# A two-layer decoder trunk on one core: a decay matrix from broadcast sums, new ranks in the planner, and weight transfers of one unit

## Chip, core and metric

The kernel runs on one core of one Trainium2 chip. The metric is the device time of one execution in microseconds; the median of three runs of the kernel before is 699.82 us (697.88 to 703.11).

## What is computed

Two decoder layers over 256 tokens of width 1024, and a last RMSNorm. All inputs are float32. Layer 0 mixes with a gated delta rule (8 heads of 64) beside a short gated convolution; layer 1 with sparse attention (16 heads, 4 groups, three branches). Each layer ends in a squared-ReLU MLP of width 4096. Of the reference, the part that the change rewrites:

```python
g = -jnp.exp(a_log) * jax.nn.softplus(a + dt_bias)          # per token and head
gc = jnp.cumsum(chunks(g), axis=-1)
decay = jnp.exp(jnp.where(incl, gc[..., :, None] - gc[..., None, :], -jnp.inf))
m_low = jnp.where(strict, jnp.einsum('nbhik,nbhjk->nbhij', kb, kc) * decay, 0.0)
u = triangular_solve(m_low + eye, vc * bc); w = triangular_solve(m_low + eye, kb * jnp.exp(gc))
attn = jnp.einsum('nbhik,nbhjk->nbhij', qc, kc) * decay
# MLP: jnp.square(jax.nn.relu(h @ w_up)) @ w_down
```

The kernel uses chunks of 128 tokens, so there are two chunks `c` and, per chunk, one decay matrix `E[c]` of 128 x 8 heads x 128.

## The kernel before

**Weights.** All weight matrices lie in one array in the order of use. `_plan` (line 50) lists them as chunks of 512 columns or their like; a chunk consists of units of [128, 1024] float32 (512 KB), the first chunk of half units, the second of units of 528 columns. `loads` (line 435) issues the transfers from SyncE's queue, two units in each, into `stage`, a pool of SB = 4 slots of [128, 2048]; a slot is filled again when both of its units have been split (flag `st`). Two half units of the first chunk share a slot. `x` and the parameter transfers stand between them at fixed positions: `rtab` ahead of transfer RT = 21, the rest of the parameters ahead of transfer P2 = 8. Two streams of `splits` (line 455) turn each unit into a rounded high half `uh` (ScalarE) and a remainder `ul` (VectorE); UB = 4 such pairs exist. The products are then hi x hi, hi x lo, lo x hi: three matmuls of 256 columns for each 128x128 block (`mm256`, line 523), 24 for a unit. `compress` (line 1533) reads its weights straight from the stage.

**The order.** The order of the instructions of every engine is made ahead of time in Python. Work is written as generator streams; at each `yield` a stream names an engine or a flag, and `Order.run` (line 250) takes the stream that can start first by a table of costs, and among equal times the one with the lowest rank (`prio`), then the oldest. `spawn` (line 178) gives a stream without a rank the rank 1 if its parent has rank MAIN (9) or SPLIT, else its parent's. SPLIT is 0 here and CHAIN, the rank of the delta rule's chain (`chain_k`, `chain_main`, `decay`), is 0 too. The stream of projections has rank 9, and -1 while a count of missed matmul columns (`debt`) is above a limit. Attention heads in layer 1 have ranks from 1 up, the ends of the norms 0. `Timed.cost` (line 299) holds the cost table: for rounded float32 the larger of 0.86 ns for each weight column and 0.46 ns for each moving column.

**Layer 0.** The projections k, (z, a, b), v, q, cg, hs, bg run in this order, then the output projection: its blocks 0 to 3 read `yb` (short convolution), 4 to 7 `ya` (delta rule). Beside them runs the chain: `decay` (line 919) makes g; `spans` (line 955) makes E; `chain_k` (line 1057) normalises k and makes `nbk`; `invert` (line 1102) makes `KB` (`keys`), the scores `al` = K KB E (`scores`), and inverts by blocks with `tt`, `uc`, `ys`; `chain_main` (line 1232) solves for x; `output` (line 1277) gives `o` and `ya`. The convolutions of q run on GpSimd, those of k and v on VectorE. The Silu activations of v, q and z wait for the flag `E1`, so that the activation table changes once.

E before: four GpSimd or VectorE products per chunk, triu times a column of g (split into two rounded parts), 128x512 each, and for each half of the heads one bfloat16 matmul that adds the mask `nleb` and two matmuls with `strictr` as weights. ScalarE takes Exp of 128x512 from PSUM.

Of the kernel before, what the change touches and what calls it, by code (L numbers as in the profile page):

```python
# [10 lines left out]
F32 = mybir.dt.float32  # L11
F32R = mybir.dt.float32r
# [8 lines left out]
T = 256  # L21
# [5 lines left out]
UN = 1024  # L27
# [4 lines left out]
FIRST, XS = (1,) * 8, ((1, 2), (2, 4), (4, 6), (6, 8))  # L32
PK, PW, PR, F1, GZ, ZP, LD, RT, P2 = 1, 0, 1, 1, 1, 1, 1, 21, 8
KPOOL, VPOOL, CVB = (), (), {'conv': 4, 'pool': 2}
CHAIN, TOK_FIRST = 0, False
TICK, BUSY = 10240 / 3, 1500.0
MAIN, SPLIT, SHARE, LIMIT, FLOOR, CAP, SPARE = 9, 0, 0.5, 300, -1500.0, 4000.0, 1
ORDER1 = ('kk', 'q0', 'kc', 'vg', 'cmp', 'q1', 'wo')


# [8 lines left out]

def _plan():  # L50

    w = UN, (2, 2)
    l1 = []
    for k in ORDER1:
        l1 += {'vg': [(560, (2,) * 4)], 'cmp': [(0, (2 * UN,) * 4)], 'wo': [w, w]}.get(k, [w])
    return [(UN // 2, FIRST), (528, (2,) * 4)] + [w] * 7 + [w] * 16 + l1 + [w] * 16


def _layout(i):
# [97 lines left out]
class Order:  # L157
# [28 lines left out]
    def flag(self, name):  # L186
        self.flags.setdefault(name, self._now())
# [62 lines left out]
    def run(self):  # L250
        while self.streams:
            best = None
            for i, s in enumerate(self.streams):
                t, at = self._start(s)
                prio = -1 if s.prio == MAIN and self.debt > self.limit else s.prio
                if t is not None and (best is None or (t, prio, i) < best[0]):
                    best = (t, prio, i), s, at
            assert best, [s.want for s in self.streams]
            _, s, at = best
            w, value = s.want, None  # L260
            if isinstance(w, (str, dict)):
                value = at
            else:
                s.hold = max(s.hold, at)
                if w[0] == 'bank':
                    slot = min(self.banks)
                    self.banks.remove(slot)
                    value = self.get_bank(slot[1])
                    self.held[id(value)] = slot[1], value
# [14 lines left out]
class Timed:  # L284
# [14 lines left out]
    def cost(self, op, a, k):  # L299
        aps = [x for x in list(a) + list(k.values()) if isinstance(x, bass.AP)]  # L300
        size = lambda x: int(np.prod(x.shape[1:]))
        if self.name != 'PE':
            return self.other(op, a, k, aps, size)
        rows = aps[1].shape[0]
        if op == 'transpose':
            return 0.85 * rows, rows * rows / 128
        m, n = size(aps[1]), size(aps[2])
        if aps[2].dtype == F32:
            if m <= 64 and aps[0].start_partition():
                return 8 + 0.7 * m, 0.0  # L310
            return max(1.75 * m, 1.68 * n), 4 * n * rows / 128
        return max((0.86 if aps[2].dtype == F32R else 0.25) * m, 0.46 * n), n * rows / 128

    def other(self, op, a, k, aps, size):
        n = max(size(x) for x in aps)
# [28 lines left out]


BANK = ('bank',)
UB, SB, SPARE1 = 4, 4, 0
SLOTS, PTS = 4, 4
WARM = 9

# [17 lines left out]
def _build(ctx, nc, tc, wts, xin, parin, out, off):  # L368
# [37 lines left out]
    pieces, units, left, raw, place = [], [], [], [], []  # L406
    at = slot = 0
    for n, split in _plan():
        fits = 2 if 0 < n * max(split) <= UN else 1
        for j in range(len(split)):  # L410
            place.append((slot + j // fits, j % fits * UN))
        slot = place[-1][0] + 1
        left += [0] * (slot - len(left))
        for per in split:
            if n:
                units += [(len(pieces), u * n, n) for u in range(per)]
            else:
# [17 lines left out]
    def loads():  # L435
        cut = off['ident'][0]
        before = {P2: [get(par[:, cut:], parin[:, cut:npar], npar - cut, 'par2')],
                  RT: [get(e.rtab, parin[:, npar:].rearrange("p (a t) -> p a t", a=2), 2 * T, 'rtab')]}
        for p, x in zip((1, 2, 3, 4), XS):
            before[p] = [load_x(*x)]  # L440
        head = [get(par[:, :cut], parin[:, :cut], cut, 'par'), load_x(0, 1)]
        before[HEAD] = head + before.get(HEAD, [])
        for p, (pos, k) in enumerate(pieces):
            for g in before.get(p, ()):
                yield from g
            slot, o = place[p]
            if not o:
                if slot >= SB:
                    yield 'flag', f'st{slot - SB}'
                st = stage.tile([128, 2 * UN], F32, name="st")  # L450
            staged[p] = st[:, o:]
            yield from get(st[:, o:o + k], bass.AP(tensor=wts.tensor, offset=wts.offset + pos, ap=[[k, 128], [1, k]]),
                           k, f'ld{p}')

    def splits(first):
        for i in range(first, len(units), 2):
            p, o, n = units[i]
            if i >= UB:
                yield 'flag', f'ud{i - UB}'
            yield 'flag', f'ld{p}'  # L460
# [36 lines left out]
    def late_consts():  # L497
        yield 'flag', 'col0'
        make = lambda nm, dt: const.tile([128, 128], dt, name=nm)
        yield 'G'  # L500
        e.strictr, e.nleb = make("strictr", F32R), make("nleb", BF16)
        e.identb, e.ngeb = make("identb", BF16), make("ngeb", BF16)
        G.tensor_copy(e.identb, ident)
        G.tensor_scalar(e.nleb, P('triu'), -1.0, -NEG, op0=OP.add, op1=OP.mult)
        G.tensor_copy(e.strictr, P('strict'))
        flag('consts')
        yield 'G'
        t = tmp.tile([128, T], F32, name="t", bufs=3)[:, :128]
# [345 lines left out]
def layer0(e, n, nxt):  # L854
# [4 lines left out]
    with ExitStack() as ctx:  # L859
# [59 lines left out]
        def decay():  # L919
# [18 lines left out]
            V.scalar_tensor_tensor(q, q, 2.0, z, op0=OP.add, op1=OP.mult)  # L938
            V.scalar_tensor_tensor(sp, sp, 0.0, q, op0=OP.max, op1=OP.add)
            V.scalar_tensor_tensor(g, sp, -1.0, ea[:, None, :].to_broadcast([128, 2, 8]), op0=OP.mult, op1=OP.mult)  # L940
            gp = [p1.tile([128, 2, 8], F32R, name=f"gp{i}", tag=t) for i, t in enumerate(("lz", "lw"))]
            V.tensor_copy(gp[0], g)
            V.tensor_sub(gp[1], g, gp[0].bitcast(F32))
            flag('g')
            spawn(spans(gp))
            b = yield BANK
            yield 'PE'
            PE.matmul(b[:, :8], triu, g[:, 1], start=True, stop=True)
            PE.matmul(b[:, 8:16], strict, g[:, 0], start=True, stop=True)
            yield 'A'  # L950
            A.activation(eg, b[:, :16], AF.Exp)
            release(b)
            flag('eg')

        def spans(gp):

            yield 'flag', 'consts'
            for c in range(2):
                parts = [m4.tile([128, 8, 128], F32R, name="gt", tag=f"m4{i}") for i in range(2)]
                E[c] = m4.tile([128, 8, 128], F32, name=f"E{c}")  # L960
                for q in range(2):
                    h = slice(4 * q, 4 * q + 4)
                    for i in range(2):
                        spawn(products(parts[i][:, h], gp[i][:, c, h], f'gt{c}{q}{i}'))
                for q in range(2):
                    b = yield BANK
                    d = view(b, 4, 128)
                    yield 'PE'
                    PE.matmul(d, e.identb, e.nleb[:, None, :].to_broadcast([128, 4, 128]), start=True, stop=False)
                    for i in range(2):  # L970
                        yield 'flag', f'gt{c}{q}{i}'
                        yield 'PE'
                        PE.matmul(d, e.strictr, parts[i][:, 4 * q:4 * q + 4], start=False, stop=(i == 1))
                    yield 'A'
                    A.activation(E[c][:, 4 * q:4 * q + 4], d, AF.Exp)
                    release(b)
                flag(f'E{c}')

        def products(dst, col, done):
            pick = yield dict(V=600, G=1076 + DBIAS)  # L980
            (V if pick == 'V' else G).tensor_mul(dst, triu[:, None, :].to_broadcast([128, 4, 128]),
                                                 col.bitcast(F32)[:, :, None].to_broadcast([128, 4, 128]))
            flag(done)


        def pool_conv(dst, pre, w, width):
# [375 lines left out]
        def bg_evac(m, acc):  # L1362
# [1 line left out]
            yield 'flag', 'E1'  # L1364
            yield 'take', 'bg', 2
            if not yb:
                yb.extend(m4.tile([128, 4, T], F32R, name="yb", tag=f"m4{a}") for a in range(2))
            yield 'V'
            t = p2.tile([128, T], F32, name="bgt", tag="lsq")
            V.tensor_mul(t, acc[:, :T], sc['cg'][:, m])  # L1370
# [33 lines left out]
def layer1(e, n, nxt):  # L1404
# [4 lines left out]
    with ExitStack() as ctx:  # L1409
# [123 lines left out]
        def compress():  # L1533
# [1 line left out]
                yield 'flag', f'blocks{i}'  # L1535
            hb = yield BANK
            for k in range(16):
                if k % 4 == 0:
                    w, done = yield from e.whole()
                yield 'PE'  # L1540
                for i in range(2):
                    o = k % 4 * 512 + i * 256
                    PE.matmul(hb[64 * i:64 * i + 64, :256], blk[i][:, k], w[:, o:o + 256], start=(k == 0),
                              stop=(k == 15))
                if k % 4 == 3:
                    flag(done)
            spawn(compressed(hb))

# [312 lines left out]
```

## Time and profile before

| | us |
|---|---|
| median of three runs | 699.82 (697.88 to 703.11) |
| the profiled execution | 699.36 |
| its span, first to last instruction | 697.6 |
| TensorE busy | 664.7 |
| VectorE busy | 479.5 |
| ScalarE busy | 388.1 |
| GpSimd busy | 136.2 |
| mean granted TensorE clock | 0.981 of full speed |

A helper records each instruction, so that all of them carry line 294; rows are told apart by the tiles' names (written tile, then read ones) and by time. Layer 0 ends at about 185 us, its MLP at about 365, layer 1 at about 515. A matmul in float32 appears as two records, one in rounded float32 or bfloat16 as one. A busy share is an average; what counts for an order is which engine waits for which at a given time.

### The profile page before, as it was taken

The numbers are of one execution on the slowest core, as the hardware profiler recorded it, in microseconds if no ns is written. First come the engines' busy times: TensorE is split into PE (matmuls) and PEld (weight loads), VectorE is DVE, ScalarE is ACT, GpSimd is POOL, SyncE is SP. The second block draws the span as 40 slices with busy tenths as digits, with TensorE's granted clock in tenths as the row PEclk, the third lists the DMA queues.
The fourth block names the chain that finished last, engine by engine and source line by source line (L and its number), as shares of the span: only waits on it lengthen the run. The fifth ranks groups of instructions, "written<-read, shape, count | busy, mean of one in ns | idle before, by whom it ended". The sixth has DMA issues, their size and how long they took to land.

```text
span 697.6 us, 15854 instructions
## 1 busy us (share of the span) xinstructions
PE 664.7 (95%) x6573; PEld 625.0 (90%) x6573; DVE 479.5 (69%) x898; ACT 388.1 (56%) x750; POOL 136.2 (20%) x177
## 2 busy tenths in 40 slices
PE   8998879996999999999999999999899999999994
PEld 6997779996999999999999876978699999999994
DVE  6999868674775556566568999997396655555452
ACT  7556223331588787444446567676478878544430
POOL 2035678100210000011013251212130000011121
PEclk9999989997999999999999999999999999999997
DMA  8843331311355555555553367213135555555501
GB/s 296 289 175 136 122 123 64 107 36 55 138 206 190 183 189 203 209 185 182 190 207 110 129 224 290 73 62 122 61 122 182 183 183 195 207 201 182 182 1 60
DMA packets 17640, 109.05 MB, mean 156 GB/s; under 512 B 2080, under 2 KB 2336, under 8 KB 5536
## 3 DMA queue, kind: packets, MB, share of 16 engines
q1 hardware_dynamic: 17280, 107.52, 44.1%
q8 instruction: 51, 0.84, 0.5%
q10 hardware_dynamic: 288, 0.52, 0.2%
q14 instruction: 21, 0.17, 0.1%
HBM read 106.99 MB, written 1.05 MB: 155 GB/s over the span
## 4 chain that ended last, share of the span: by engine, by line
PE 75%; DVE 16%; issue 3%; ACT 3%; DMA 1%; SPq 0%; POOL 0%; DVEq 0%; ACTq 0%; POOLq 0%
PE b L294 75%; DVE ul L294 4%; DVE cvconv L294 1%; DVE x L294 1%; ACT uh L294 1%; DVE kc L294 1%; DMA X<-xt 1%; DVE swq L294 1%; DVE rqt L294 1%; DVE X L294 1%; DVE nm L294 0%; ACT px L294 0%; DVE lc L294 0%; DVE qr L294 0%; DVE cm L294 0%
## 5 line engine op out<-in xcount | busy, mean ns | idle before, releaser
L294 DVE TENSOR_TENSOR ul<-st,uh 128x1024 fp32r<-128x1024 f32 (+3 forms) x204 | 244.2, 1200 | 143.4 <-ACT uh L294 141.1
L294 ACT ACTIVATE uh<-st 128x1024 fp32r<-128x1024 f32 (+3 forms) x204 | 205.8, 1011 | 195.3 <-PE b L294 179.6
L294 PE MATMUL b<-x,uh 128*128 128x256 f32 (+1 forms) x1632 | 295.5, 283 | 2.0 <-DVE x L294 0.8
L294 PEld LDWEIGHTS b<-x,uh 128*128 128x128 f32 x1632 | 249.4, 189 | 6.6 <-ACT uh L294 1.8
L294 PE MATMUL b<-x,ul 128*128 128x256 f32 x832 | 231.1, 279 | 0.7 <-DVE ul L294 0.6
L294 PE MATMUL b<-U,uh 128*128 128x256 f32 x1024 | 174.2, 276 | 0.0
L294 PEld LDWEIGHTS b<-x,ul 128*128 128x128 f32 x832 | 157.1, 189 | 1.8 <-DVE ul L294 1.5
L294 PEld LDWEIGHTS b<-U,uh 128*128 128x128 f32 x1024 | 154.1, 188 | 0.0
L294 PE MATMUL b<-U,ul 128*128 128x256 f32 x512 | 141.3, 276 | 0.0
L294 PEld LDWEIGHTS b<-U,ul 128*128 128x128 f32 x512 | 96.1, 188 | 0.0
L294 POOL TENSOR_TENSOR nacc<-nacc,sq 128x256 f32<-128x256 f32 x24 | 27.1, 1127 | 244.2 <-ACT sq L294 244.1
L294 ACT ACTIVATE px<-b,nm 128x128 f32<-128x128 f32 (+1 forms) x64 | 26.3, 423 | 10.0 <-DVE nm L294 9.7
L294 ACT ACTIVATE U<-u 128x256 fp32r<-128x256 f32 x64 | 26.8, 419 | 2.0
L294 ACT ACTIVATE u<-t 128x256 f32<-128x256 f32 x64 | 26.7, 418 | 2.0
L294 POOL TENSOR_TENSOR px<-px,den 128x128 f32<-128x128 f32 x32 | 17.3, 568 | 53.5 <-DVE den L294 39.1
L294 DVE TENSOR_TENSOR U<-u,U 128x256 fp32r<-128x256 f32 x64 | 27.0, 425 | 0.7 <-ACT U L294 0.7
L294 PE MATMUL b<-uh,x 128*128 128x264 f32 (+1 forms) x128 | 24.9, 290 | 0.0
L294 POOL TENSOR_TENSOR X<-X,par 128x256 f32<-128x256 f32 x8 | 5.5, 694 | 99.2 <-ACT nacc L294 90.2
L294 PE MATMUL b<-ohl,uh 128*128 128x256 f32 x128 | 24.6, 291 | 0.2
L294 ACT ACTIVATE t<-b 128x256 f32<-128x256 f32 x64 | 23.3, 364 | 0.0
L294 DVE SCALAR_TENSOR_TENSOR x<-X,par,x 128x256 fp32r<-128x256 f32 x32 | 19.1, 616 | 4.2 <-ACT x L294 4.1
L294 PEld LDWEIGHTS b<-ohl,uh 128*128 128x128 f32 x128 | 19.6, 189 | 0.9 <-ACT ohl L294 0.3
(274 smaller groups left out, 806.0 us busy)
## 6 DMA issues: line engine op xcount, KB each, us to landing
st<-wts SPq DMA_DIRECT2D x94, 1024.0 KB, 4.8
st<-wts SPq DMA_DIRECT2D x4, 560.0 KB, 3.7
st<-wts SPq DMA_DIRECT2D x4, 528.0 KB, 4.8
st<-wts SPq DMA_DIRECT2D x8, 256.0 KB, 5.4
X<-xt SPq DMA_DIRECT2D x3, 256.0 KB, 5.4
par<-par SPq DMA_DIRECT2D x1, 525.0 KB, 5.8
out_dram<-X SPq DMA_DIRECT2D x2, 256.0 KB, 2.6
out_dram<-X ACTq DMA_DIRECT2D x2, 256.0 KB, 3.1
```

What stands on the lines that cost most here:

```text
L294: r = f(*a, **k)
```

## The change

- E is built otherwise. The column of g for one head, broadcast over 128 columns, is the weights of a float32 matmul with triu as moving operand: every row then holds the running sum of g. The mask matmul stays. Exp is taken head by head with the negated running sum of the row as bias (`ngk`, made by one small ScalarE operation). The products, `strictr` and the split of g go. The two small matmuls for `eg` become one of 16 columns and one of 8. Four `spans` streams are spawned by `decay`.
- The outputs `yb` of the short convolution no longer share their place with the products.
- Ranks: `splits` sets its rank to 0 for the first 16 units and to SPLIT = 0.5 after; so `spawn` now gives the children of rank-0 streams the rank 0. A table YIELD of zeros is added to the start times.
- The cost of a rounded float32 matmul in the planner becomes the larger of 0.885 ns for each weight column and 0.443 ns (up to 256 columns; 0.455 above) for each moving column.
- Each transfer is one unit, and the stage has eight slots of one unit. Two half units of the first chunk share a slot of one unit.

```diff
-MAIN, SPLIT, SHARE, LIMIT, FLOOR, CAP, SPARE = 9, 0, 0.5, 300, -1500.0, 4000.0, 1
+CHAIN, EARLY, TOK_FIRST = 0, 16, False
+YIELD = (0.0, 0.0, 0.0)
+MAIN, SPLIT, SHARE, LIMIT, FLOOR, CAP, SPARE = 9, 0.5, 0.5, 300, -1500.0, 4000.0, 1
...
-    w = UN, (2, 2)
+    w = UN, (1,) * 4
...
-        l1 += {'vg': [(560, (2,) * 4)], 'cmp': [(0, (2 * UN,) * 4)], 'wo': [w, w]}.get(k, [w])
-    return [(UN // 2, FIRST), (528, (2,) * 4)] + [w] * 7 + [w] * 16 + l1 + [w] * 16
+        l1 += {'vg': [(560, (1,) * 8)], 'cmp': [(0, (UN,) * 8)], 'wo': [w, w]}.get(k, [w])
+    return [(UN // 2, FIRST), (528, (1,) * 8)] + [w] * 7 + [w] * 16 + l1 + [w] * 16
...
-        return max((0.86 if aps[2].dtype == F32R else 0.25) * m, 0.46 * n), n * rows / 128
+        return max((0.885 if aps[2].dtype == F32R else 0.25) * m, (0.443 if n <= 256 else 0.455) * n), n * rows / 128
...
-UB, SB, SPARE1 = 4, 4, 0
+UB, SB, SPARE1 = 4, 8, 0
...
-        fits = 2 if 0 < n * max(split) <= UN else 1
+        fits = 2 if 0 < n * max(split) <= UN // 2 else 1
         for j in range(len(split)):
-            place.append((slot + j // fits, j % fits * UN))
+            place.append((slot + j // fits, j % fits * (UN // 2)))
...
-                st = stage.tile([128, 2 * UN], F32, name="st")
+                st = stage.tile([128, UN], F32, name="st")
...
             p, o, n = units[i]
+            order.cur.prio = 0 if i < EARLY else SPLIT
...
-            gp = [p1.tile([128, 2, 8], F32R, name=f"gp{i}", tag=t) for i, t in enumerate(("lz", "lw"))]
-            V.tensor_copy(gp[0], g)
-            V.tensor_sub(gp[1], g, gp[0].bitcast(F32))
-            flag('g')
-            spawn(spans(gp))
             b = yield BANK
             yield 'PE'
-            PE.matmul(b[:, :8], triu, g[:, 1], start=True, stop=True)
-            PE.matmul(b[:, 8:16], strict, g[:, 0], start=True, stop=True)
+            PE.matmul(b[:, :16], triu, g.rearrange("p c h -> p (c h)"), start=True, stop=True)
+            PE.matmul(b[:, 16:24], strict, g[:, 0], start=True, stop=True)
             yield 'A'
-            A.activation(eg, b[:, :16], AF.Exp)
+            ngk = small("ngk", 2, 8)
+            A.activation(ngk.rearrange("p c h -> p (c h)"), b[:, :16], AF.Copy, scale=-1.0)
+            A.activation(eg, b[:, 8:24], AF.Exp)
...
+        def spans(c, q, ngk):
+            b = yield BANK
+            d = view(b, 4, 128)
+            yield 'PE'
+            PE.matmul(d, e.identb, e.nleb[:, None, :].to_broadcast([128, 4, 128]), start=True, stop=False)
+            for j in range(4):
+                yield 'PE'
+                PE.matmul(d[:, j], g[:, c, 4 * q + j:4 * q + j + 1].to_broadcast([128, 128]), triu,
+                          start=False, stop=(j == 3))
+            for j in range(4):
+                yield 'A'
...
+                A.activation(E[c][:, h], d[:, j], AF.Exp, bias=ngk[:, c, h:h + 1])
+            release(b)
...
-                yb.extend(m4.tile([128, 4, T], F32R, name="yb", tag=f"m4{a}") for a in range(2))
+                yb.extend(m4.tile([128, 4, T], F32R, name=f"yb{a}") for a in range(2))
...
-                if k % 4 == 0:
+                if k % 2 == 0:
                     w, done = yield from e.whole()
```

## Rows read from the trace of the kernel before

**Rows 1.** The page, engine totals: busy us, share, instructions.
```profile
PE 664.7 (95%) x6573; PEld 625.0 (90%) x6573; DVE 479.5 (69%) x898; ACT 388.1 (56%) x750; POOL 136.2 (20%) x177
```

**Rows 2.** Stages: stretch, its length, busy us (records) by engine, clock, DMA share, GB/s.
```profile
40.00:70.00 30.00, 26.92 (x213) 24.93 (x214) 28.79 (x63) 16.73 (x30) 15.50 (x13) 1.00 0.34 116
70.00:92.00 22.00, 18.22 (x328) 17.08 (x330) 20.07 (x48) 4.84 (x6) 13.92 (x17) 1.00 0.40 139
92.00:102.00 10.00, 7.54 (x213) 6.81 (x213) 4.00 (x9) 1.89 (x3) 7.76 (x11) 0.66 0.18 41
...
164.00:178.00 14.00, 8.59 (x45) 7.80 (x44) 5.91 (x15) 3.23 (x4) 1.26 (x1) 0.63 0.22 75
```

**Rows 3.** Waits of TensorE, 0 to 180 us: total us, times, longest.
```profile
PE b L294 <- issue: 2.5, 1, 2.5
PE b L294 <- DVE ys L294: 1.9, 1, 1.9
```

**Rows 4.** Order of time, TensorE: start, us, instruction, [idle before, and releaser].
```profile
168.70 1.08 PE L294 MATMUL b<-par,o 128*128 128x128 f32 x4 [4.58 <-DVE o L294]
170.47 1.31 PE L294 MATMUL b<-ya,uh 128*128 128x256 f32 x2 [0.69 <-ACT ya L294]
```

**Rows 5.** Order of time, the chain's start, on VectorE and TensorE.
```profile
54.50 1.01 DVE L294 SCALAR_TENSOR_TENSOR nbk<-beta,rk 128x16 f32<-128x16 f32 x1
57.25 1.06 PE L294 MATMUL b<-par,wide 128*128 128x128 f32 x8 [1.53 <-DVE preconv L294]
71.27 1.27 DVE L294 TENSOR_TENSOR KB<-K,b 128x512 f32<-128x512 f32 x2
78.61 2.15 DVE L294 SCALAR_TENSOR_TENSOR al<-b,rk,E 128x128 f32<-128x128 f32 x8
83.43 0.75 PE L294 MATMUL b<-tt,al 32*32 32x32 f32 x64 [1.42 <-DVE tt L294]
86.47 0.45 DVE L294 STREAM_TRANSPOSE uc<-tt 128x256 f32<-128x256 f32 x1
86.84 1.18 DVE L294 TENSOR_TENSOR ul<-st,uh 128x1024 fp32r<-128x1024 f32 x1
```

**Rows 6.** Instructions of the products' tile: ns min/median/max, first and last start.
```profile
L294 POOL TENSOR_TENSOR gt<-par,gp x8: 1036/1132/2025, 45.0 to 56.4; 128x512 fp32r<-128x512 f32 x8
```

**Rows 7.** Groups by shape, VectorE, 45 to 58 us: busy us, mean ns, idle before.
```profile
L294 DVE TENSOR_TENSOR ul<-st,uh 128x1024 fp32r<-128x1024 f32 x4 | 6.1, 1550 | 0.0
L294 DVE SCALAR_TENSOR_TENSOR cvconv<-preconv,par,cvconv 128x256 f32<-128x256 f32 x2 | 2.6, 1292 | 0.0
```

**Rows 8.** The tile `ul` on VectorE, 200 to 360 us.
```profile
L294 DVE TENSOR_TENSOR ul<-st,uh x60: 1220/1226/1228, 199.1 to 359.3; 128x1024 fp32r<-128x1024 f32 x60
```

**Rows 9.** Order of time, VectorE, one tap of a convolution.
```profile
59.27 0.47 DVE L294 SCALAR_TENSOR_TENSOR cvconv<-preconv,par,cvconv 128x256 f32<-128x256 f32 x1
```

**Rows 10.** Order of time, TensorE, the scores of the first chunk.
```profile
72.09 2.02 PE L294 MATMUL b<-KB,K 64*128 64x128 f32 x16 [0.41 <-DVE KB L294]
```

**Rows 11.** Groups by shape, ScalarE, whole span: busy us, mean ns, idle before.
```profile
L294 ACT ACTIVATE px<-b,nm 128x128 f32<-128x128 f32 x32 | 11.4, 366 | 9.4 <-DVE nm L294 9.3
L294 ACT ACTIVATE E<-b 128x512 f32<-128x512 f32 x4 | 2.2, 586 | 1.3 <-PE b L294 1.3
```

**Rows 12.** Stages of 10 us, at the start and in the first MLP.
```profile
10.00:20.00 10.00, 9.45 (x74) 8.85 (x75) 8.82 (x26) 6.91 (x17) 3.14 (x5) 1.00 0.97 349
...
300.00:310.00 10.00, 10.00 (x91) 10.00 (x90) 6.06 (x7) 4.77 (x6) 0.92 (x1) 1.00 0.56 197
```

**Rows 13.** The tile `st` on SyncE's queue: issue ns, and us from issue to landing.
```profile
L426 SPq DMA_DIRECT2D st<-wts x110: 327/328/665, 1.6 to 656.0; - x110
...
DMA to landing us min/median/max: 3.2/4.8/8.9
```

**Rows 14.** Waits of ScalarE, 0 to 60 us: total us, times, longest.
```profile
ACT uh L294 <- DMA st<-wts: 1.1, 2, 0.6
```

More of the change, by code (lines that the diff above doesn't have):

```diff
@@ L34 @@
 KPOOL, VPOOL, CVB = (), (), {'conv': 4, 'pool': 2}
-CHAIN, TOK_FIRST = 0, False
+CHAIN, EARLY, TOK_FIRST = 0, 16, False
+YIELD = (0.0, 0.0, 0.0)
 TICK, BUSY = 10240 / 3, 1500.0
-MAIN, SPLIT, SHARE, LIMIT, FLOOR, CAP, SPARE = 9, 0, 0.5, 300, -1500.0, 4000.0, 1
+MAIN, SPLIT, SHARE, LIMIT, FLOOR, CAP, SPARE = 9, 0.5, 0.5, 300, -1500.0, 4000.0, 1
 ORDER1 = ('kk', 'q0', 'kc', 'vg', 'cmp', 'q1', 'wo')
@@ L255, in run @@
                 prio = -1 if s.prio == MAIN and self.debt > self.limit else s.prio
-                if t is not None and (best is None or (t, prio, i) < best[0]):
-                    best = (t, prio, i), s, at
+                if t is not None:
+                    key = t + (0.0 if isinstance(s.want, tuple) else YIELD[min(int(prio), 2)]), prio, i
+                    if best is None or key < best[0]:
+                        best = key, s, at
             assert best, [s.want for s in self.streams]
@@ L500, in late_consts @@
         yield 'G'
-        e.strictr, e.nleb = make("strictr", F32R), make("nleb", BF16)
+        e.nleb = make("nleb", BF16)
         e.identb, e.ngeb = make("identb", BF16), make("ngeb", BF16)
@@ L504, in late_consts @@
         G.tensor_scalar(e.nleb, P('triu'), -1.0, -NEG, op0=OP.add, op1=OP.mult)
-        G.tensor_copy(e.strictr, P('strict'))
         flag('consts')
@@ L950, in decay @@
+            PE.matmul(b[:, 16:24], strict, g[:, 0], start=True, stop=True)
             yield 'A'
-            A.activation(eg, b[:, :16], AF.Exp)
+            ngk = small("ngk", 2, 8)
+            A.activation(ngk.rearrange("p c h -> p (c h)"), b[:, :16], AF.Copy, scale=-1.0)
+            A.activation(eg, b[:, 8:24], AF.Exp)
             release(b)
             flag('eg')
-        def spans(gp):
             yield 'flag', 'consts'
             for c in range(2):
-                parts = [m4.tile([128, 8, 128], F32R, name="gt", tag=f"m4{i}") for i in range(2)]
-                E[c] = m4.tile([128, 8, 128], F32, name=f"E{c}")
@@ L961, in spans @@
                 for q in range(2):
[L962 to L976, printed above, removed]
@@ L977, in spans @@
-                flag(f'E{c}')
[L979 to L983, printed above, removed]
+                    spawn(spans(c, q, ngk))
+        spread = {}
+        def spans(c, q, ngk):
[9 more added lines that the diff above has]
+                yield 'A'
+                if E[c] is None:
+                    E[c] = m4.tile([128, 8, 128], F32, name=f"E{c}")
+                h = 4 * q + j
+                A.activation(E[c][:, h], d[:, j], AF.Exp, bias=ngk[:, c, h:h + 1])
+            release(b)
+            spread[c] = spread.get(c, 0) + 1
+            if spread[c] == 2:
+                flag(f'E{c}')
@@ L1541, in compress @@
                 for i in range(2):
-                    o = k % 4 * 512 + i * 256
+                    o = k % 2 * 512 + i * 256
                     PE.matmul(hb[64 * i:64 * i + 64, :256], blk[i][:, k], w[:, o:o + 256], start=(k == 0),
                               stop=(k == 15))
-                if k % 4 == 3:
+                if k % 2:
                     flag(done)
```

## The prediction

> **What bounds the kernel now.** Read first the page's engine line: TensorE is busy in 95% of the span [rows 1], so the whole kernel holds some 33 us in which it stands. Read then the table by stage [rows 2]. Each row gives, for a stretch of layer 0, the busy time of each engine and the granted clock. In 40 to 70 us TensorE stands 3.1 us and VectorE is busy 28.8 of 30 us: VectorE sets the pace there, since it makes the low half of every weight unit and empties every PSUM bank of the projections. In 70 to 92 TensorE stands 3.8 us, in 92 to 102 2.5 us, in 164 to 178 5.4 us. That is 14.8 us in layer 0 after the start, the largest part of what can be won by a different order. Two of these rows also show a granted clock below 1: 0.66 and 0.63. The clock has two levels, 1.2 and 2.4 GHz, so a mean of 0.66 over 10 us is 6.8 us at the lower one, and 0.63 over 14 us is 10.4 us. In both TensorE had stood before.
>
> The list of waits names what ended the standing: 2.5 us for nothing the profile shows, 1.9 us for `ys` of VectorE [rows 3]. The longest stands in the order of time before the transposes of `o`, 4.6 us up to 168.70, and is followed by 0.7 us for `ya` [rows 4]. This is the end of the delta rule's chain (decay matrix E, inversion by blocks, solve, output): the projections had run out, and the second half of the output projection needs `ya`. So in layer 0 two limits alternate: VectorE's load up to about 90 us, and the chain's length at its end.
>
> The chain starts late. `nbk` is made at 54.50, but `KB`, which needs only it and one group of transposes, runs on VectorE at 71.27, and the first inversion step at 83.43 [rows 5]. Between them stand convolutions and weight splits, which the planner ranks no lower: with SPLIT = 0, a stream that a rank-0 stream spawns gets rank 1 (`spawn`, line 181), so `invert`, `chain_q`, `spans` and `output` have rank 1, below the splits at 0.
>
> **The change, part by part.** *Decay matrix.* Eight products of 128x512 on GpSimd go [rows 6]. They cost more than GpSimd's time, which nobody lacks: VectorE's instructions beside them are stretched. Between 45 and 58 us four `ul` took 1.55 us on the mean, two taps of the convolution 1.29 [rows 7], where they take 1.23 and 0.47 elsewhere [rows 8, 9]. The excess is 4 x 0.32 + 2 x 0.82 = 2.9 us, by these two groups alone, on an engine that is full there. The Trainium skill, "SBUF — State Buffer", section "SBUF: two separate sides", says that GpSimd and a VectorE operation with two SBUF inputs share one port pair as a lock, held for a whole instruction. By that rule eight products of 1.13 us could hold VectorE up to 9.1 us; the trace agrees in kind, and its smaller size is what I use.
>
> On TensorE, eight matmuls of 512 columns in the rounded format go. 91 of 256 columns fill 10 us in the MLP [rows 12], 0.11 each, so 0.22 for 512 and 1.8 us in all. Sixteen fp32 matmuls of 128x128 with a spread column of g as weights come. The nearest is `KB` x K: a chunk's eight matmuls, seen as 16 records, took 2.02 us, 0.25 each [rows 10]; sixteen are 4.0 us. The net is +2.2 us of TensorE, on the path, since TensorE is nearly full. Bounds: 0 if all of it falls into standing time, 4.0 if nothing that goes was on the path. ScalarE replaces four Exp of 128x512 at 0.59 by sixteen of 128x128; the nearest row, with an accumulator, took 0.37 [rows 11], so at most +3.5 us. ScalarE is busy 16.7 of 30 us there [rows 2], so this is hidden; without that cover E would come up to 3.5 us later, which matters only from `scores` on. The negated sum and the merged small matmul are one 16-column operation more: nothing.
>
> *Ranks.* SPLIT becomes 0.5 for units from 16 on. Splits now give way to the chain, and what the chain spawns keeps rank 0. `KB` can follow its transposes, which end at 58.3 [rows 5], instead of standing at 71: the chain starts 13 us earlier, more if VectorE's stretched instructions ahead of `nbk` go too. It has to come only some 6 us earlier for the final wait to go. What goes with it: 4.6 + 0.7 us of waiting, and the lower clock behind it. Of the 10.4 us at the lower level in 164 to 178 it stood at most 5.3, and it was busy 8.6 us in all, so 5.1 to 8.6 us ran at half speed and 2.6 to 4.3 us are lost; I take 3.2. Term: -8.5. If another wait takes its place it is 0. In the middle, the 1.9 us for `ys` stand behind a 1.2 us `ul`, which ended just before it [rows 5]: splits no longer go first, -1.9 (bounds 0 and all of 70 to 102: 3.8 + 2.5 of standing, and 3.1 for the clock, from the 6.8 us at the lower level less a part of the standing: -9.4). In 40 to 70, relief of VectorE should give half of the 3.1 us: -1.5 (bounds 0 and -3.1).
>
> Against this: the chain's VectorE work is moved ahead of splits and evacuations where VectorE is full. It is `KB` 1.3, the first chunk's eight `al` some 2.1 (as the second's), and 78.61 to 86.92 for the second's and both chunks' transposes and masks, 8.3 [rows 5]: 11.7 us. TensorE holds four split units of 24 matmuls, 10.6 us at 0.11. It starves for 1.1 us: +1.1 (bounds 0 and 11.7).
>
> *The planner's matmul cost* falls from 0.46 to 0.443 ns a column for 256 columns, 118 to 113 ns, nearer to the 110 of [rows 12]. It only reorders: 0, with 3 us to either side for the order in layer 1. There the splits stay ahead of attention (rank 1 and more); only the norms' ends (rank 0) now pass them.
>
> *Transfers.* 110 issues [rows 13] become 212: each pair becomes two, the eight half units stay. At 0.33 us the 102 more take 34 us of SyncE's queue, which spends most of its time waiting for a slot; hidden. Without that cover each unit would come 0.33 us later. The stage holds eight units as before, and a slot is free after one split instead of two. At the start the half units now fill four slots of eight, so that four of the 264 KB pieces go out without a wait. ScalarE waited 1.1 us in all for weights up to 60 us [rows 14]; what of it reaches TensorE is small: 0 (bounds -1.1 and 0). `rtab` (256 KB) moves from behind eighteen units of layer 0 to behind five: 0.7 us at the 349 GB/s of [rows 12], hidden by eight staged units, at most +0.7.
>
> Sum: -8.5 - 1.9 - 1.5 + 2.2 + 1.1 = -8.6. The profiled execution took 699.4 us (span 697.6 and 1.8 around it), 0.4 below the median of 699.8, so I make no correction: 690.8, rounded 691.
>
> **The rivals.** *The gain is paid back (within 1%).* The final wait is replaced by another: `output` also needs `attn`, and so Q, whose convolutions run on GpSimd at rank 1 and now come later; or starving costs 5 us. Then -8.5 shrinks to about -2: 697. For it: VectorE is full and total work stays. Against: the chain needs only 6 of its 13 us. Also here: the order barely moves, because a static plan hides it, and only the matmuls stay: 699.4 + 2.2 = 702.
>
> *Starvation (slower).* In 45 to 70 us, all 11.7 us of moved VectorE work becomes standing time of TensorE, and it drops to the lower level after it, as the rows at 92 and 164 show, for 3.1 us more. With the final wait gone: 11.7 + 3.1 + 2.2 - 8.5 = +8.5, 708. It decides from 13 us of new standing and clock loss on. For it: the banks of the projections are emptied by VectorE too. Against: four units are in store, and the chain's own matmuls fill some of the time.
>
> *More goes than I count.* All 14.8 us of standing and 6.3 of clock go, less 2.2: -18.9, 680.5. Against: the 2.5 us without a visible cause will hardly follow from rank.
>
> *Transfers too small (slower).* If one transfer at a time were on its way and half a MB landed no sooner than a pair does on the median, 4.8 us [rows 13], each of the 128 units of the MLPs, eaten in 24 x 0.11 = 2.6 us, would add 2.2: +280, about 980. It begins where a unit takes over 2.6 us. Against it stands the start of the trace, where transfers of 128 to 528 KB reached 349 GB/s at 0.97 of the engines, while the MLP asks for 197 [rows 12]: several overlap, and eight slots leave 21 us for one to land. The Trainium skill, "DMA: Bandwidth & Descriptors", section "Bandwidth", asks for batches of 1 MiB or more, which speaks against this change; by the 2.0 us plus bytes over 436 GB/s of its section "Anatomy of one DMA" half a MB takes 3.2 us, an estimate from that page, and one at a time would add some 75 us.
>
> **How the numbers follow.** Forecast (686 to 695): 0.48. More goes (680 to 686): 0.11. Paid back or not moved (695 to 702): 0.25. Starvation: 0.13. Transfers: 0.03. About 1%, 7 us, is what a measurement of this kernel can tell from no change. Of the forecast some 0.04 lies within it. Faster by over 1%: 0.48 + 0.11 - 0.04 = 0.55; within 1%: 0.25 + 0.04 = 0.29; slower: 0.13 + 0.03 = 0.16. The range 681 to 704 leaves out most of starvation, the transfers and the tip of the best case.
>
> **What would show it.** `KB` before 62 us and the first inversion step before 72; no wait of TensorE above 2 us for `o` or `ya`; the granted clock in the last 15 us of layer 0 at 1.00; `ul` at 1.23 us around 50 us; sixteen matmuls of E in some 4 us; 212 loads, and no wait of ScalarE for `st` in either MLP. I would be wrong if TensorE stands over 5 us between 45 and 75 us, if the output's wait stays with another releaser, or if layer 1's order loses what layer 0 gains.

## The result, and the profile after

| | before | after |
|---|---|---|
| median, us | 699.0 (697.88 to 703.11) | 690.52 (688.98 to 691.10) |
| runs | 4 | 4 |
| profiled execution, us | 699.36 | 688.98 |
| its span, us | 697.6 | 687.1 |

The ratio is 0.9875, with an interval of 0.9844 to 0.9907: the kernel is 8.5 us faster. The forecast was 691.0, and the gain 8.6. In the profiled pair it is 10.4.

The engine totals, where [rows 1] stood:

```profile
PE 663.2 (97%) x6597; PEld 628.4 (91%) x6597; DVE 466.2 (68%) x885; ACT 395.3 (58%) x773; POOL 124.1 (18%) x169
```

TensorE now stands 23.9 us of its span where it stood 32.9. Where the time went shows in the two tiles that layers 0 and 1 end with, the output projections' `ya` and `ohl`. In the rows of a tile, the columns are shortest, median and longest duration in ns and the first and the last start in us.

```profile
L297 PE MATMUL b<-ya,ul x32: 279/281/283, 162.6 to 173.6; 128*128 128x256 f32 x32
...
L297 PE MATMUL b<-ohl,ul x64: 276/280/287, 454.7 to 499.4; 128*128 128x256 f32 x64
```

The same two rows of the kernel before:

```profile
L294 PE MATMUL b<-ya,ul x32: 276/276/420, 171.6 to 184.4; 128*128 128x256 f32 x32
...
L294 PE MATMUL b<-ohl,ul x64: 276/276/284, 462.7 to 509.7; 128*128 128x256 f32 x64
```

So layer 0 gained 10.8 us, and the stretch from there to the end of layer 1 lost 0.5 (325.8 instead of 325.3). What follows took 187.7 instead of 187.9. All of the gain lies in layer 0. Its stages after the change, in the columns of [rows 2]:

```profile
40.00:70.00 30.00, 29.71 (x467) 28.36 (x466) 28.21 (x84) 15.90 (x36) 2.14 (x2) 1.00 0.35 111
70.00:102.00 32.00, 27.04 (x833) 24.68 (x821) 23.67 (x48) 8.75 (x14) 22.45 (x29) 0.95 0.41 115
145.00:175.00 30.00, 29.57 (x246) 28.86 (x245) 22.00 (x40) 13.05 (x19) 3.61 (x3) 1.00 0.52 159
```

In 40 to 70 us TensorE stands 0.3 us (3.1 before), in 70 to 102 5.0 us (6.2 before, at a lower clock), and in the last 30 us of the layer 0.4 us, at full clock. VectorE is as full as before between 40 and 70 (28.2 of 30 us), but with other work. GpSimd's 15.5 us there are 2.1. The waits of TensorE in 0 to 180 us, total, times and longest, where [rows 3, 4] stood:

```profile
PE b L297 <- issue: 5.0, 4, 2.8
...
PE b L297 <- DVE ya L297: 0.4, 1, 0.4
PE b L297 <- DVE KB L297: 0.3, 1, 0.3
```

The 4.6 us for `o` and the 1.9 for `ys` are gone. The chain's start, from VectorE and, in the last line, TensorE in order of time (start, duration), where [rows 5] stood:

```profile
46.14 1.23 DVE L297 TENSOR_TENSOR ul<-st,uh 128x1024 fp32r<-128x1024 f32 x1
47.29 0.17 DVE L297 SCALAR_TENSOR_TENSOR nbk<-beta,rk 128x16 f32<-128x16 f32 x1
...
51.00 1.28 DVE L297 TENSOR_TENSOR KB<-K,b 128x512 f32<-128x512 f32 x2
...
64.39 0.75 PE L297 MATMUL b<-tt,al 32*32 32x32 f32 x64
```

`nbk` comes 7.2 us earlier and takes 0.17 us where it took 1.01. `KB` follows it after 3.7 us where 16.8 lay between. The first inversion step stands at 64.4 instead of 83.4. Last, the new parts themselves: TensorE's matmuls of E by line and shape (count | busy us, mean ns | idle before), ScalarE's Exp, and the loads. A float32 matmul is two records, so the 32 are sixteen matmuls.

```profile
L297 PE MATMUL b<-par,g 128*128 128x128 f32 x32 | 4.2, 275 | 0.0
```
```profile
L297 ACT ACTIVATE E<-b,ngk x16: 349/392/453, 46.7 to 51.8; 128x128 f32<-128x128 f32 x16
```
```profile
L429 SPq DMA_DIRECT2D st<-wts x212: 327/328/653, 1.6 to 645.7; - x106
```

### The profile page after: what moved, and what is told of

It reads as the page before. It is cut to its first block, busy times and chain, and to the rows that moved or that the text cites. A ratio compares the mean times of both kernels' runs of the same rounds, so it can differ in the third digit from the quotient of the medians.

```text
span 687.1 us, 16191 instructions
## 1 busy us (share of the span) xinstructions
PE 663.2 (97%) x6597; PEld 628.4 (91%) x6597; DVE 466.2 (68%) x885; ACT 395.3 (58%) x773; POOL 124.1 (18%) x169
## 4 chain that ended last, share of the span: by engine, by line
PE 84%; DVE 9%; issue 3%; DMA 2%; ACT 2%; SPq 0%; DVEq 0%; ACTq 0%
PE b L297 84%; DVE ul L297 3%; DMA st<-wts 2%; DVE cvconv L297 1%; ACT uh L297 1%; DVE kc L297 1%; SPq L429 0%; DVE KL L297 0%; DVE swq L297 0%; DVE nm L297 0%; DVE t L297 0%; DVE rqt L297 0%; DVE qr L297 0%; DVE X L297 0%; DVE nacc L297 0%
## 5 line engine op out<-in xcount | busy, mean ns | idle before, releaser
L297 DVE TENSOR_TENSOR ul<-st,uh 128x1024 fp32r<-128x1024 f32 (+3 forms) x204 | 241.5, 1187 | 149.5 <-ACT uh L297 147.5
L297 POOL TENSOR_TENSOR nacc<-nacc,sq 128x256 f32<-128x256 f32 x24 | 28.2, 1175 | 245.8 <-ACT sq L297 245.6
L297 ACT ACTIVATE px<-b,nm 128x128 f32<-128x128 f32 (+1 forms) x64 | 26.3, 430 | 11.7 <-DVE nm L297 10.8
L297 PE MATMUL b<-uh,x 128*128 128x264 f32 (+1 forms) x128 | 28.0, 308 | 3.9 <-DVE t L297 2.7
L297 PEld LDWEIGHTS b<-uh,x 128*128 128x128 f32 x128 | 22.2, 202 | 4.5 <-issue 2.9
L297 POOL TENSOR_TENSOR px<-px,den 128x128 f32<-128x128 f32 x32 | 15.9, 525 | 46.4 <-DVE den L297 32.3
```

The source lines that it names most:

```text
L297: r = f(*a, **k)
```

## The experiments

Twelve kernels. Most change one part of four: the decay matrix, the ranks, the transfers, the planner's matmul cost. In the table KB is the start of `KB` and "end of layer 0" the start of the last matmul of `ya`; before, they are 71.3 and 184.4. Ratios are against the kernel before on the same chip, whose median was 699.7 us for the first four rows, 698.2 for the next four and 700.6 for the last four.

| kernel | median, us | ratio | KB | end of layer 0 |
|---|---|---|---|---|
| before + ranks (b_ranks) | 696.31 | 0.9975 [0.9928, 1.0023] | 52.2 | 180.6 |
| before + decay matrix (b_decay) | 689.65 | 0.9862 [0.9806, 0.9919] | 53.7 | 173.6 |
| before + transfers (b_trans) | 700.13 | 0.9997 [0.9966, 1.0028] | 71.8 | 186.1 |
| before + matmul cost (b_cost) | 717.05 | 1.0254 [1.0191, 1.0317] | 75.7 | 202.0 |
| after without ranks (a_noranks) | 687.01 | 0.9830 [0.9788, 0.9873] | 55.0 | 170.7 |
| after without decay matrix (a_nodecay) | 691.66 | 0.9897 [0.9854, 0.9940] | 51.6 | 175.8 |
| after without transfers (a_notrans) | 699.49 | 0.9994 [0.9953, 1.0034] | 51.3 | 172.7 |
| after without cost (a_nocost) | 688.55 | 0.9844 [0.9790, 0.9898] | 51.7 | 176.5 |
| b_decay + unplanned products (d_pool_free) | 695.27 | 0.9912 [0.9875, 0.9950] | 58.0 | 178.2 |
| b_decay + planned products (d_pool_plan) | 709.67 | 1.0133 [1.0075, 1.0190] | 70.1 | 193.7 |
| before, products on VectorE (b_prodV) | 699.64 | 0.9985 [0.9959, 1.0011] | 59.9 | 185.0 |
| before + decay + transfers (b_decay_trans) | 687.30 | 0.9793 [0.9751, 0.9835] | 52.8 | 171.8 |

**The ranks alone.**

```diff
-MAIN, SPLIT, SHARE, LIMIT, FLOOR, CAP, SPARE = 9, 0, 0.5, 300, -1500.0, 4000.0, 1
+MAIN, SPLIT, SHARE, LIMIT, FLOOR, CAP, SPARE = 9, 0.5, 0.5, 300, -1500.0, 4000.0, 1
...
+            order.cur.prio = 0 if i < EARLY else SPLIT
```

> The kernel before with the ranks alone (splits 0.5 from unit 16 on, so the chain's children keep rank 0). Theory 1, the ranks move the chain forward and so take away the final wait for o: about -8 us against before, KB near 58 us instead of 71, no wait of TensorE over 2 us for o or ya. Theory 2, the new decay matrix is what moves it (VectorE's stretched instructions and late E): -2 to 0 here, KB still after 62 us. Theory 3, any new order of the planner gives a few us either way: between -5 and +5 without a clear mark in the chain.

The mechanism came as forecast and the time did not. `KB` stands at 52.2 and no wait for `o` is left, yet the ratio can't be told from 1. From b_ranks, first the tile `KB`, then TensorE's waits in 0 to 190 us, then one stage:

```profile
L294 DVE TENSOR_TENSOR KB<-K,b x2: 681/685/689, 52.2 to 52.8; 128x512 f32<-128x512 f32 x2
```
```profile
PE b L294 <- DVE ys L294: 5.3, 3, 1.9
PE b L294 <- DVE tt L294: 3.8, 2, 3.3
```
```profile
70.00:100.00 30.00, 22.12 (x684) 20.96 (x685) 23.19 (x58) 6.10 (x9) 17.76 (x23) 0.83 0.24 77
```

In 70 to 100 us TensorE stands 7.9 us, mostly for the inversion's own steps `ys` and `tt`, and a granted clock of 0.83 means that a third of that stage ran at the lower level. Layer 0 ends 3.8 us earlier instead of 8.5.

**The decay matrix alone.** The hunks of `decay`, `spans` and `yb` of the diff above, with the old ranks, transfers and cost; its core:

```diff
-                        spawn(products(parts[i][:, h], gp[i][:, c, h], f'gt{c}{q}{i}'))
...
+                    spawn(spans(c, q, ngk))
...
+                PE.matmul(d[:, j], g[:, c, 4 * q + j:4 * q + j + 1].to_broadcast([128, 128]), triu,
+                          start=False, stop=(j == 3))
```

> The kernel before with the new decay matrix alone. Theory 1: VectorE's relief is worth -1.5 and TensorE's added work +2.2, so -1 to +2 us, and KB stays late (65 to 71 us), since its rank is still 1. Theory 2: -6 us or more, KB before 60. Theory 3: between -5 and +5.

It came as theory 2 had it. This one part gives as much as the whole change: 0.9862 against 0.9875, intervals over each other, and a layer 0 that ends at 173.6 as there. (The places of their own for `yb` go with it; they were not tried alone, but before the products' tile was last read at 60 us and `yb` first written at 117, so no `yb` can have waited for it.) VectorE of b_decay in order of time; the bracket is the idle time before and what ended it:

```profile
48.24 0.17 DVE L294 TENSOR_TENSOR rqt<-rqt,s 128x16 f32<-128x16 f32 x1
...
49.64 0.17 DVE L294 SCALAR_TENSOR_TENSOR nbk<-beta,rk 128x16 f32<-128x16 f32 x1
...
53.67 1.28 DVE L294 TENSOR_TENSOR KB<-K,b 128x512 f32<-128x512 f32 x2 [0.59 <-PE b L294]
```

With the old ranks `KB` still has the lower claim on VectorE, and yet it goes the moment its transposes are there: VectorE even stands 0.59 us for them. So the old rank by itself does not hold it back. In the kernel before it had a VectorE against it that stood 0.4 us in all between 54.5 and 71.3; either a better rank (b_ranks) or the products' going (b_decay) moves it.

**The transfers alone.** The hunks of `_plan`, the stage and `compress`; their core:

```diff
-    w = UN, (2, 2)
+    w = UN, (1,) * 4
...
-UB, SB, SPARE1 = 4, 4, 0
+UB, SB, SPARE1 = 4, 8, 0
```

> The kernel before with transfers of one unit into eight slots alone. Theory 1 and 2: within 1 us of before, no wait of ScalarE for st in an MLP, twice the issues at 0.33 us. If transfers of half the size landed too slowly, TensorE would stand in both MLPs and the time would grow by tens of us. Theory 3: between -5 and +5, since load times enter the planner.

No effect on the median. The final wait stays, as the wait list of b_trans shows:

```profile
PE b L294 <- DVE o L294: 6.6, 1, 6.6
```

The ten runs lie within 1.1 us, where eighteen of the nineteen of the kernel before beside them lie within 8.5 (697.0 to 705.5; the last took 709.8). The size of the transfers alone does not set this: four runs of a_nocost, with units, spread over 5.7 us, ten of b_prodV, with pairs, over 3.3. In after a unit's DMA lands 4.3 us after its issue on the median, a pair before 4.8 [rows 13]. The Trainium skill, "DMA: Bandwidth & Descriptors", section "Bandwidth", asks for 1 MiB and more in a transfer to come to 75% of the peak. Here half of that cost nothing, with eight slots ahead.

**The matmul cost alone.**

```diff
-        return max((0.86 if aps[2].dtype == F32R else 0.25) * m, 0.46 * n), n * rows / 128
+        return max((0.885 if aps[2].dtype == F32R else 0.25) * m, (0.443 if n <= 256 else 0.455) * n), n * rows / 128
```

> The kernel before with the planner's new matmul cost alone (0.443 in place of 0.46 ns a column). Theory 1: within 3 us of before, sign open. Theory 2: 0. Theory 3: between -5 and +5; if the truer cost itself matters, -3 or better.

Put at nothing, it costs 17 us on the old kernel, which no theory allowed: 3.7% off an entry of a table that only the planner reads. Wait list and one stage of b_cost:

```profile
PE b L294 <- DVE o L294: 6.6, 1, 6.6
PE b L294 <- ACT Vf L294: 3.5, 1, 3.5
```
```profile
160.00:190.00 30.00, 20.17 (x151) 17.72 (x152) 13.08 (x36) 5.28 (x9) 1.26 (x1) 0.50 0.00 1
```

The order that it gives has `KB` at 75.7, and near the end of layer 0 30 us in which TensorE stands 9.8 us and is granted the lower level throughout. The 30 us hold next to no DMA and no wait of TensorE there names a load or a split: what is late is the chain. Why this order is so much worse was not followed further.

**The same four taken out of after, one at a time.** First SPLIT goes back to 0.

```diff
-MAIN, SPLIT, SHARE, LIMIT, FLOOR, CAP, SPARE = 9, 0.5, 0.5, 300, -1500.0, 4000.0, 1
+MAIN, SPLIT, SHARE, LIMIT, FLOOR, CAP, SPARE = 9, 0, 0.5, 300, -1500.0, 4000.0, 1
```

> The kernel after with SPLIT back at 0 (no ranks). Theory 1, the ranks carry the gain: about 698, KB after 62 us, the wait for o at layer 0's end is back. Theory 2, the decay matrix carries it: 690 to 693. Theory 3: between 688 and 700 with no clear mark.

Then the products come back in place of the head-by-head matmuls.

```diff
-                    spawn(spans(c, q, ngk))
...
+                        spawn(products(parts[i][:, h], gp[i][:, c, h], f'gt{c}{q}{i}'))
```

> The kernel after with the decay matrix of before (GpSimd's products). Theory 1: 690 to 693, KB before 62 us, VectorE stretched again beside the products. Theory 2: 697 or more. Theory 3: between 688 and 700.

Then the pairs and their four slots.

```diff
-    w = UN, (1,) * 4
+    w = UN, (2, 2)
...
-UB, SB, SPARE1 = 4, 8, 0
+UB, SB, SPARE1 = 4, 4, 0
```

> The kernel after with transfers of pairs into four slots. Theory 1 and 2: 690 to 692. Theory 3: between 688 and 696.

Last, the old cost.

```diff
-        return max((0.885 if aps[2].dtype == F32R else 0.25) * m, (0.443 if n <= 256 else 0.455) * n), n * rows / 128
+        return max((0.86 if aps[2].dtype == F32R else 0.25) * m, 0.46 * n), n * rows / 128
```

> The kernel after with the planner's old matmul cost. Theory 1 and 2: 688 to 694. Theory 3: between 688 and 698.

Without the ranks the kernel gets faster, not slower, and more so than any theory had it: 0.9830, and layer 0 ends 2.9 us before that of after. The stage at 70 us in a_noranks, to be held against the second window of after:

```profile
70.00:102.00 32.00, 30.95 (x835) 29.34 (x823) 24.32 (x47) 10.16 (x16) 22.68 (x28) 1.00 0.49 137
```

TensorE stands 1.1 us there instead of 5.0, at full clock, with `KB` 4 us later. So once the chain is early enough, pulling it further forward gains nothing. What it costs in after are not waits for the chain's steps: all 5.0 us are waits that the profile puts down to nothing, and the last section says what they are. The intervals of the two ratios overlap, so the 0.5% is likely rather than certain; the other pair that differs in the ranks alone (b_decay_trans 0.9793, a_nocost 0.9844) says the same, with intervals that overlap too.

Without the decay matrix 0.9897 remains: beside the other three parts it is worth 0.2%, alone 1.4%. Either the ranks or the decay matrix brings `KB` to 51 to 55 us; for the chain's start they are substitutes, and the second to come finds nothing left to gain. For the time this is shown in part only: the ranks gain no clear time alone, and the 1% of a_nodecay is that of ranks, transfers and cost together. The old cost in after gives 0.9844, not told apart from 0.9875: what ruined the old order by 2.5% does not matter to the new one.

Without the transfers all of the gain goes, which no theory had: 0.9994. Layer 0 is as good as in after (172.7); the profile, at 695.21 us among the shorter of its ten runs (694.5 to 703.7), loses 7 us in layer 1 (332.8 instead of 325.8). TensorE's waits of a_notrans from 180 to 515 us, and the stage:

```profile
PE b L297 <- DVE t L297: 2.6, 1, 2.6
PE b L297 <- ACT pts L297: 2.0, 3, 0.9
PE b L297 <- DVE qr L297: 1.9, 1, 1.9
```
```profile
355.00:505.00 150.00, 139.78 (x1041) 116.41 (x1041) 118.83 (x286) 93.50 (x265) 35.54 (x64) 0.97 0.34 122
```

After is busy 144.93 us of these 150. Which part of this is a different order and which the transfers themselves was not separated, and the spread of its runs stays open too.

**Is it the collision or the order?** The products went from GpSimd, and `KB` moved 18 us. Two things can do that: VectorE's instructions are no longer stretched on the chip, or the planner, whose `spend` sets a VectorE instruction with two SBUF inputs behind a GpSimd instruction that it overlaps, now makes another order. Two kernels put eight products of 128x512 back into b_decay, on work that nobody reads. In the first the planner does not know of them, and the orders of TensorE, VectorE and ScalarE are those of b_decay; in the second it does.

```diff
+                        spawn(extra(c, q, scratch))
...
+        def extra(c, q, scratch):
+            yield 'flag', 'eg'
+            nc.gpsimd.tensor_mul(scratch, triu[:, None, :].to_broadcast([128, 4, 128]),
+                                 g[:, c, 4 * q:4 * q + 4, None].to_broadcast([128, 4, 128]))
```

The planned form has `yield 'G'` and `G.tensor_mul` in their place.

> The kernel before with the new decay matrix, and eight GpSimd products of 128x512 put in where the old ones stood, with results nobody reads, and unseen by the planner: every other engine keeps the order of b_decay. It prices the collision of GpSimd and VectorE by itself. Theory A, the stretched VectorE instructions are the price: 3 to 6 us above b_decay's 689.7, ul and small operations stretched around 46 to 56 us. Theory B, the planned order is what counts: 690 to 691, the stretch is hidden.

> The same eight products, known to the planner, which holds VectorE's time back for them. Theory A: as with the unseen ones, 693 to 696. Theory B, a fuller VectorE in the plan lets older work of equal rank go before KB: KB after 60 us again and 695 to 700, well above the unseen ones.

Unplanned, they show the bare collision. VectorE of d_pool_free in order of time, then GpSimd's products as a tile, then `KB`, then the longest wait of TensorE:

```profile
48.43 0.81 DVE L294 TENSOR_SCALAR rk<-s 128x16 int32<-128x16 int32 x1
49.28 0.17 DVE L294 TENSOR_TENSOR rqt<-rk 128x16 f32<-128x16 f32 x1
49.49 0.90 DVE L294 TENSOR_TENSOR rqt<-rqt,s 128x16 f32<-128x16 f32 x1
50.43 0.17 DVE L294 SCALAR_TENSOR_TENSOR rqt<-rqt 128x16 f32<-128x16 f32 x1
50.63 0.90 DVE L294 SCALAR_TENSOR_TENSOR rk<-rqt,rk 128x16 f32<-128x16 f32 x1
...
53.86 0.16 DVE L294 SCALAR_TENSOR_TENSOR nbk<-beta,rk 128x16 f32<-128x16 f32 x1
```
```profile
L986 POOL TENSOR_TENSOR scratch<-par,g x8: 1062/1067/2002, 44.9 to 53.9; 128x512 fp32r<-128x512 f32 x8
```
```profile
L294 DVE TENSOR_TENSOR KB<-K,b x2: 681/682/683, 58.0 to 58.6; 128x512 f32<-128x512 f32 x2
```
```profile
PE b L294 <- ACT wide L294: 3.6, 1, 3.6
```

Every second small instruction is held until a product ends: 0.8 to 0.9 us where b_decay took 0.17. The one at 49.49, for instance, ends at 50.39, and a product ran from 49.29 to 50.36. `nbk` and `KB` come 4.2 and 4.3 us later than in b_decay, TensorE waits 3.6 us for the transposes' input, and the span is 4.5 us longer (691.1 and 686.6). By the ratios it is 0.5%, 3.5 us; their intervals overlap, so the time is likely only, while the delay of the chain stands in the traces. Planned, `KB` and the last wait are those of the kernel before again (tile, then wait list, of d_pool_plan):

```profile
L294 DVE TENSOR_TENSOR KB<-K,b x2: 677/677/677, 70.1 to 70.7; 128x512 f32<-128x512 f32 x2
```
```profile
PE b L294 <- DVE o L294: 4.6, 1, 4.6
```

At 709.67 us it lies above both figures expected. That is 2.7% over b_decay, 19 us, of which the collision alone explains 4. The rest is order: against d_pool_free, measured beside it, 14 us. The order of d_pool_plan is not that of the kernel before, so the split holds in kind and not in size.

**No collision, but the work on VectorE.** All eight products of the kernel before go to VectorE.

```diff
-            pick = yield dict(V=600, G=1076 + DBIAS)
+            pick = yield 'V'
```

> The kernel before with all eight products on VectorE in place of GpSimd. Theory A, the collision keeps the chain late: KB near 55 us, faster than before by 3 us or more. Theory B, VectorE's load decides when KB, the youngest work of its rank, gets a turn: eight products of 0.7 us more on VectorE, KB at 66 us or later, 698 to 703.

`KB` at 59.9 met neither figure, and nothing is gained. The tile `gt` of b_prodV, and its longest wait:

```profile
L294 DVE TENSOR_TENSOR gt<-par,gp x8: 651/682/920, 55.7 to 82.1; 128x512 fp32r<-128x512 f32 x8
```
```profile
PE b L294 <- DVE o L294: 4.2, 1, 4.2
```

The products drag on to 82 us, so E is late, and the scores with it. An early `KB` is not enough: both of the chain's inputs have to be early. TensorE made E in 4.2 us; VectorE took until 82 us to find room for it.

**The decay matrix and the transfers together,** with the old ranks and cost: the two diffs of b_decay and b_trans in one kernel.

```diff
-    w = UN, (2, 2)
+    w = UN, (1,) * 4
...
+                    spawn(spans(c, q, ngk))
```

> The kernel before with the new decay matrix and the transfers of one unit, without ranks and without the new matmul cost. If ranks and cost bring nothing once the decay matrix is there: 684 to 690, as good as or better than the kernel after (690.5) and the one without ranks (687.0). If the four parts need each other: 691 or more. Runs should spread by about 2 us, as those of all kernels with transfers of one unit so far.

At 0.9793 it is the lowest ratio measured, with a_noranks (0.9830) beside it; by the ratios they lie 0.8% and 0.5% below after, and the first of these two intervals lies clear of that of after. Its four runs spread by 3.0 us.

## Why the prediction came out, point by point

The sum was -8.6 and 8.5 was measured. That they agree to 0.1 us is luck: in the profiled pair layer 0 alone gained 10.8 us, the runs of the kernel before lie 5 us apart, and two of the four parts together took time away. That the gain fell into the range is more than luck, since most of the signs came: `KB` at 51.0 (before 62 forecast), the first inversion step at 64.4 (before 72), no wait above 2 us for `o` or `ya` (0.4), the clock of the layer's end at 1.00, `ul` at 1.23 us around 50 us, 212 loads, no wait of ScalarE for weights in the MLPs, and layer 1 at +0.5 us where ±3 was allowed. So place and mechanism were right: a chain that starts late makes a wait at the end of the layer, and the wait goes when the chain starts 20 us earlier.

- **Ranks: the step that failed.** The working gives the -8.5 of the final wait and its clock to the ranks, because the inversion stood behind splits of a better rank [rows 5]. The ranks alone do move `KB`, but pay only 3.8 us by the end of layer 0 and nothing that the timing can tell from 0. The decay matrix alone moves `KB` as far at the old rank and pays all. What held `KB` was a VectorE that had fallen behind, on the chip and in the plan; rank decides only while older work of a better rank is ready.
- **VectorE's relief, mis-sized.** It stood at -1.5, half of what TensorE stood in 40 to 70 us; of those 3.1 us 0.3 remain. The excess behind it was 2.9 us, read from two groups of large instructions [rows 7 to 9]. Left out were the small ones of the norm of k, which lead straight to `nbk`. The kernel before has them too (VectorE in order of time):

```profile
48.45 0.81 DVE L294 TENSOR_SCALAR rk<-s 128x16 int32<-128x16 int32 x1
49.30 0.97 DVE L294 TENSOR_TENSOR rqt<-rk 128x16 f32<-128x16 f32 x1
...
51.35 0.96 DVE L294 SCALAR_TENSOR_TENSOR rk<-rqt,rk 128x16 f32<-128x16 f32 x1
```

  With `nbk` at 1.01 [rows 5] these four lose some 3.1 us against 0.17 each, on the chain's own path. The relief measured alone is some 3.5 to 4.5 us (d_pool_free against b_decay), and what the planner makes of it is more than that again. The prediction let only the ranks change the order; the removed products changed it as well.
- **E's price right.** E's matmuls took 4.2 us (4.0 forecast). The sixteen Exp took 0.39 us each (0.37 from the nearest row), hidden on ScalarE.
- **The middle: the wait went, the standing stayed.** The 1.9 us for `ys` went as forecast, but of the 6.2 us that TensorE stood in 70 to 102 us 5.0 remain. All of it is of the kind without a visible cause, of which the prediction said that it "will hardly follow from rank"; it grew from 2.5 us to 5.0.
- **Starvation did not come.** It was priced for 45 to 70 us, where TensorE in fact stands 0.3 us. In b_ranks it stands 7.9 us between 70 and 100 us, at a clock of 0.83, but for the inversion's own `ys` and `tt`, not for split units. That kernel came out where "paid back" had put it, 696.3 us for 697, with other waits than that rival named.
- **Matmul cost: wrong alone, right here.** At "0, 3 us to either side" it was 17 us on the old order. On the new one it cannot be told from 0. The bound of 3 had no row behind it.
- **Transfers: 0 on the median of the old kernel, as forecast.** That after needs them (0.9994 without) was not in the sum at all.

The single effects do not add: 0.9975, 0.9862, 0.9997 and 1.0254 give a product of 1.008, and together they measured 0.9875. One order in which each step is measured is transfers 0.9997, with the decay matrix 0.9793, with the ranks 0.9844, with the cost 0.9875. By it the decay matrix brings 2%, and the other two give back about 0.8% of it; how the 0.8% divides between them the intervals do not tell. The total was met because one cause (the chain's late start) was sized from what it cost, 8.5 us [rows 2, 4], and not from the part that was believed to lift it.

## What to carry to other kernels

Size a gain by the wait that would go, but test each part of a bundle alone before crediting it: parts that lift the same wait replace each other, and the second can cost. Where the order is made by a planner, an entry of its cost table or a removed instruction moves everything behind it, and "it only reorders" cost 17 us here. Work put on an idle engine isn't free when it holds up a full one; look at the small instructions on the path, not only at the large ones with much busy time.

## What the runs showed of the hardware

- Beside GpSimd products of 1.07 us, every second one of VectorE's instructions of 128x16 took 0.81 to 0.90 us in d_pool_free, and 0.17 without them: one is held until a product ends, the next slips in before the following product starts. In the kernel before four of them took 0.81 to 1.01 us. The prediction's guess from large instructions was of 0.3 to 0.8 us each. The Trainium skill, "SBUF — State Buffer", section "SBUF: two separate sides", describes such an exclusive lock on a shared port pair, held for a whole instruction; d_pool_free agrees. Over eight products, which ran from 44.9 to 54.9 us, it held `KB` up 4.3 us.
- A wait that the profile puts down to nothing ("issue"): TensorE stands 2.8 us inside a batch of 64 matmuls of 32x32, with 14 left. After, in order of time:

```profile
72.92 0.32 PE L297 MATMUL b<-tt,al 32*32 32x32 f32 x14 [2.77 <-issue]
```

  The fourteen traces hold 28 such waits of over 0.15 us, and they keep to a grid: from one to the next there are always 128 matmuls or a multiple of it, to within a few records. With their weight loads 128 matmuls are 256 instructions. Each wait ends 1.2 to 1.6 us after a packet of 16,384 bytes has landed on the queue that the profile calls "q8 instruction". After, from each of its four waits to the next (stretch, length, TensorE's busy us with its matmuls, clock, DMA share, GB/s), then that queue (packets, MB, share):

```profile
72.92:82.13 9.21, 8.08 (x256) 0.81 0.38 113
82.13:95.47 13.34, 12.48 (x384) 1.00 0.30 82
95.47:100.19 4.72, 4.54 (x127) 1.00 0.41 115
```
```profile
q8 instruction: 52, 0.85, 0.5%
```

  TensorE's 6597 matmuls and as many loads make 51.5 times 256, and the queue has 52 packets; before, 6573 make 51.4 times, and it has 51. The packet ahead of the longest wait (70.14 to 72.92 us) landed at 71.43. So the traces say that TensorE waits there for its own instructions: all 28 lie between 70 and 132 us, where the inversion's short matmuls use them up quickly. No kernel was made to try it. The waits are 5.0 us between 70 and 102 us in after, all that TensorE stands there, 2.5 us in the kernel before [rows 3], 0.3 us in a_noranks and nothing in b_ranks. Behind the longest the clock was 0.81 for 9.2 us. Why one order meets them more than another was not followed.
- Halving the transfers left the median of the kernel before as it was (0.9997). The runs of b_trans lay closer together, but those of other kernels with units did not all; no run tells why.
